# Two spare tiles in on-chip memory, and the first modulations on TensorE, in a two-block network on one core

## The chip, the core and the metric

The kernel runs on one core of a Trainium2 chip. TensorE (PE) does the matmuls, VectorE (DVE) and ScalarE (ACT) the elementwise work, GpSimd (POOL) a little of it, and SyncE (SP) issues nearly all transfers from one queue in program order. The metric is the device time of one execution in microseconds (us), lower is better. Before: median 3408.51 us of three runs (3404.82 to 3412.46).

## The reference

512 tokens of width 1024 pass through two blocks in float32. Every layer is modulated by a conditioning vector `c`: each needs a product of one vector with a 1024 x 3072 (first block) or 1024 x 6144 (second block) matrix before its activations can be scaled.

```python
def _modulation(c, w, b):
    m = jax.nn.silu(c) @ w + b
    shift, scale, gate = jnp.split(m, 3, axis=-1)
    return shift[:, None, :], scale[:, None, :], gate[:, None, :]

def first_block(...):
    for i in range(DEPTH):                       # DEPTH = 2
        shift, scale, gate = _modulation(c, mix_ada_w[i], mix_ada_b[i])
        h = x * (1.0 + scale) + shift
        y = _sgu_pool_mixer(h, ...) if i % 2 == 0 else _conformer_conv(h, ...)
        x = _layer_norm(DEEPNORM_ALPHA * x + (1.0 + gate) * y, mix_ln_g[i], mix_ln_b[i])
        shift, scale, gate = _modulation(c, ffn_ada_w[i], ffn_ada_b[i])
        h = x * (1.0 + scale) + shift
        y = _conv_ffn(h, ffn_w_up[i], ffn_dw[i], ffn_dw_b[i], ffn_w_down[i])
        x = _layer_norm(DEEPNORM_ALPHA * x + (1.0 + gate) * y, ffn_ln_g[i], ffn_ln_b[i])
    return x
# second_block: RWKV + windowed attention, then neighbourhood + global attention, with an FFN
# (width 4096) after each, modulated by six chunks each of silu(c_2) @ w_ada and silu(c_ctx_2) @ w_ada
```

The first mixer, `_sgu_pool_mixer`, projects to `u`, `v` and `z`, mixes `v` along the tokens, pools `z` over windows, and projects back.

## The kernel before

**Matmuls.** Activations are kept transposed (`hThi`, `hTlo`: 128 channels by 512 tokens for each of 8 channel groups). Every float32 product is taken in three fp32r matmuls, high by high, high by low and low by high (`mm3`, L304 to L308), and so each weight tile exists as `wraw` (as loaded), `whi` and `wlo` (pool `wp`). The names of the product's output tell the stage: `vps`, `ups`, `zps` and `dnps` in the first mixer, `upps` and `dnps` in the FFNs of block one, `cvps` and `cvacc` in the second mixer (`cvacc`: the depthwise convolution as matmuls with diagonal weights `dg`, 31 taps of three matmuls, each tap's moving operand starting 4 bytes further on), `up2ps` in block two.

**Where tiles lie.** Tiles are placed one behind the other in each partition's memory in the order in which pools make them. As the program is built, `whi`, `wlo` and `wraw` start 160 bytes past a multiple of 256, `hThi`, `hTlo` and the FFN's hidden tiles (`hidh`, `hidl`) 128 past one, `dg` 128 past one. A row names out <- moving operand, stationary operand: in `zps`, `ups`, `upps` and `up2ps` the activations move and the weights stand, in `vps` and `dnps` the weights move, and in `cvacc` the activations (`zh`, `zl`) move and `dg` stands.

**The modulations.** Before the first mixer can scale its input, `ada_first` (L251) computes shift and scale for the first half of the channels (q=0) and then for the second (q=1): four parts of 512 columns, each from two raw tiles of 1 MB (`adaw`, three in rotation). For a raw tile DVE multiplies four 128x512 slices by a per-partition scalar and adds them up (`ada_rows`, L202 and L204), and then TensorE sums over partitions with four 128x1 matmuls (`adaps`, L209). The other modulations of block one and those of block two are cut into pieces of 256 columns (`ada_piece`, two raws of 512 KB, two `adaw` buffers, three sums `adacc`), which are mixed into the stream by `fill()`: each call takes one entry of `todo` (L784). Twelve pieces lie in the first mixer: the gate of the mixer, then shift, scale and gate of the first FFN. SP issues a piece's transfer when its buffer is free, and every later transfer waits behind it.

Of the kernel before, what the change touches and what calls it, by code (L numbers as in the profile page):

```python
# [1 line left out]

# [3 lines left out]

# [5 lines left out]
F32 = mybir.dt.float32  # L12
# [9 lines left out]
D = 1024  # L22
KD = 8
# [19 lines left out]
class Consts:  # L43


    def __init__(self):
        self.parts, self.at, self.n = [], {}, 0
# [11 lines left out]
def host_consts():  # L59
    c0, c1, c2, c3, c4, c5, c6 = (Consts() for _ in range(7))  # L60
    p = np.arange(128)
    c0.put("ident", np.eye(128))
    c0.put("one", np.ones((128, 1)))
    c0.put("ones5", np.ones((128, 128)))
    c0.put("head", np.stack([p < 64, p >= 64], 1))

    c1.put("ones", np.ones((128, 128)))
    ic = np.ones((4, 2, 8), np.float32)
    for g, w in enumerate(WINDOWS):
        h = w // 2  # L70
        t = np.arange(S)
        c = (np.minimum(t + h, S) - np.maximum(t - h, 0)).astype(np.float32)
        ic[g, 0] = np.float32(1) / c[:8]
        ic[g, 1] = np.float32(1) / c[-8:]
    c1.put("ic", np.repeat(ic.reshape(1, 64), 128, 0))

    f = p % 64
    inv = (np.float32(ROPE_BASE) ** (-np.arange(16, dtype=np.float32) / np.float32(16))).astype(np.float32)
    t = np.arange(S)
    pos = np.where((f < 32)[:, None], t[None] // GRID_W, t[None] % GRID_W).astype(np.float32)  # L80
    ang = (pos * inv[f % 16][:, None]).astype(np.float32).astype(np.float64)
    c3.put("cos", np.cos(ang))
    c3.put("sin", np.sin(ang))
    perm = np.zeros((128, 128))
    for m in range(128):
        if m % 32 < 16:
            perm[m + 16, m] = -1
        else:
            perm[m - 16, m] = 1
    c3.put("perm", perm)  # L90

    q, k = np.arange(128)[:, None], np.arange(128)[None]
    c2.put("prev", np.where(k >= q, 0, NEG))
    c2.put("next", np.where(k <= q, 0, NEG))

    t, u = (p % 64)[:, None], np.arange(64)[None]
    c4.put("eye", t == u)
    c4.put("mn0", u < t)
    c4.put("mn1", u > t)
    c4.put("mq0", t <= u)  # L100
    c4.put("mq1", t >= u)
    c4.put("dg", t // 16 == u // 16)
    c4.put("lo", np.concatenate([(t // 16 > u // 16) & (p[:, None] // 64 == q) for q in range(2)], 1))
    c4.put("dg2", p[:, None] // 16 == p[None] // 16)

    c6.put("reset", np.repeat(np.arange(T2)[None] % 64 != 0, 128, 0))
    c6.put("heads", p[:, None] // 64 == p[None] // 64)

    t = p % 64
    c5.put("colmask", np.where((np.arange(64)[None] >= np.clip(t - 8, 0, 48)[:, None])  # L110
                               & (np.arange(64)[None] < np.clip(t - 8, 0, 48)[:, None] + 16), 0, NEG))
    return [c0, c1, c2, c3, c4, c5, c6]
# [7 lines left out]
class Kernel:  # L120
# [3 lines left out]
    todo = []  # L124
# [5 lines left out]
    def __init__(self, tc, ap, consts):  # L130
        self.tc, self.nc, self.ap = tc, tc.nc, ap
        self.consts = consts
        self.es = ExitStack()
        self.const = self.pool("const")
        self.wp = self.pool("wp")
        self.small = self.pool("small")
        self.nacc = self.pool("nacc")
        self.vp2 = self.pool("vec2")
        self.hp = self.pool("hT")
        self.vec, self.c = {}, {}  # L140
        self.load_consts(0, self.const)

    def pool(self, name, es=None, **k):
        return (es or self.es).enter_context(self.tc.tile_pool(name=name, bufs=1, reuse_waits="tile", **k))
# [44 lines left out]
    def silu_cols(self, name, vecs):  # L189
# [3 lines left out]
            self.nc.scalar.activation(t[:, m], v, AF.Silu)  # L193
        return t

    def ada_rows(self, acc, raw, sil, m, h):

        v = self.nc.vector
        for k in range(4):
            s = sil[:, m, h + k:h + k + 1]  # L200
            if h + k == 0:
                v.tensor_scalar(acc, raw[:, k, :], s, None, op0=MUL)  # L202
            else:
                v.scalar_tensor_tensor(acc, raw[:, k, :], s, acc, op0=MUL, op1=ADD)  # L204
# [6 lines left out]
    def ada_piece(self, w, sil, c0, dst, ms, buf, sums):  # L211
# [17 lines left out]
                nc.vector.tensor_copy(dst[:, ms[0]:ms[0] + n, c0 // 128:c0 // 128 + 2], t)  # L229
        return [partial(part, 0), partial(part, 4)]  # L230

    def ada_load(self, d, bias, pool):

        _, m, n = d.shape
        c = pool.tile([128, m, n], F32, tag=f"mod{m}{n}", name="mod", bufs=2)
        self.nc.vector.tensor_tensor(c, d, bias[:, None, :].to_broadcast([128, m, n]), ADD)
        return c
# [13 lines left out]
    def ada_first(self, w, sil, bias):  # L251

        nc = self.nc
        big = self.nacc.tile([128, 3, 4, 512], F32, tag="nacc", name="adaw0")
        m = self.vp.tile([128, 2, KD], F32, name="m0")
        i = 0
        for q in range(2):
            for x in range(2):
                acc = self.tmp("adacc0")
                c0 = D * x + 512 * q  # L260
                for h in (0, 4):
                    raw, i = big[:, i % 3], i + 1
                    nc.sync.dma_start(raw, w[128 * h:128 * h + 512, c0:c0 + 512].rearrange("(k p) c -> p k c", p=128))
                    self.ada_rows(acc, raw, sil, 0, h)
                t = self.ps.tile([128, 4], F32, tag="tr", name="adaps", bufs=2)
                self.ada_sums(t, acc)
                k = slice(4 * q, 4 * q + 4)
                nc.vector.tensor_tensor(m[:, x, k], t, bias[:, KD * x + 4 * q:KD * x + 4 * q + 4], ADD)
                if x == 1:
                    nc.vector.tensor_scalar(m[:, x, k], m[:, x, k], 1.0, None, op0=ADD)  # L270
            yield m
# [461 lines left out]
    def block1(self, xd):  # L733
        nc, ap = self.nc, self.ap
# [7 lines left out]
        adaw = lambda: self.act.tile([128, 4, 256], F32, tag="adaw", name="adaw", bufs=2)  # L742
        adaw()
        self.tmp("first", S + 16)
        x = self.act.tile([128, NT, D], F32, name="x")
        self.cols("a", [("c", ap["c"]), ("c2", ap["c_2"]), ("cc2", ap["c_ctx_2"])] + [(f"mix_b{i}", ap["mix_ada_b"][i]) for i in range(2)])
        sil = self.silu_cols("silc", [self.vec["c"]])
        self.sil2 = sil2 = self.silu_cols("sil2", [self.vec["c2"], self.vec["cc2"]])
        sums = lambda n: [self.vp.tile([128, 256], F32, tag="adacc", name="adacc", bufs=3) for _ in range(n)]
        ada1 = [self.vp.tile([128, 1, 3 * KD], F32, name=f"ada1_{k}") for k in range(4)]  # L750
        rows1 = self.tc.dram_tile([4, 1, D], F32, name="gates1")
        self.rows2 = self.tc.dram_tile([2, 2, 2, D], F32, name="gates2")
        self.ada_d = [self.vp2.tile([128, 2, 6 * KD], F32, name=f"ada2_{i}") for i in range(2)]
        V = self.vec
        first = self.ada_first(ap["mix_ada_w"][0], sil, V["mix_b0"])
        ws = []
        for q in range(2):
            m0 = next(first)
# [8 lines left out]
        n = x  # L767
        phases = [(i, part) for i in range(2) for part in ("mix", "ffn")]

        def ada(k, *qs):  # L770
            i, part = phases[k]
            pieces = [self.ada_piece(ap[f"{part}_ada_w"][i], sil, 512 * q + c, ada1[k], (0,), adaw, sums) for q in qs for c in (0, 256)]
            return [lambda p=p: [f() for f in p] for p in pieces]

        ada2 = [f for c in range(24) for f in self.ada_piece(ap["w_ada_2"][0], sil2, 256 * c, self.ada_d[0], (0, 1), adaw, sums)]

        def columns():
# [3 lines left out]
            self.cols("e", [("cv_dw", ap["cv_dw"]), ("cv_db", ap["cv_dw_b"]), ("cv_lng", ap["cv_ln_g"]),  # L781
                            ("cv_lnb", ap["cv_ln_b"])])

        todo = [ada(0,4,5)+[columns]+ada(1,0,1)+["gate"]+ada(1,2,3)+["mod"],  # L784
                ada(1, 4, 5) + ["gate"] + ada(2, 0, 1, 2, 3) + ["mod"] + ada(2, 4, 5) + ada(3, 0, 1, 2, 3, 4, 5) + ada2[:14],
                ["gate", "mod"],
                ["gate"] + ada2[14:] + self.begin2()]
        for k, (i, part) in enumerate(phases):
# [4 lines left out]
            rows = self.rows_gb(ap[f"{part}_ln_g"][i], ap[f"{part}_ln_b"][i])  # L793
            gate = self.act.tile([128, D], F32, tag="gate", name="gate", bufs=1)
# [23 lines left out]
            f = (lambda *a: self.ffn1(i, *a)) if part == "ffn" else (partial(self.mixer0, ws), self.mixer1)[i]  # L818
            n = f(hT, done, gate, x)
# [1165 lines left out]
```

## Time and profile before

| | before |
|---|---|
| median of three runs | 3408.51 us |
| the profiled execution | 3406.89 us |
| its span, first to last instruction | 3405.1 us |
| mean granted TensorE clock | 0.956 of 2.4 GHz |
| PE busy | 3149.5 us, 92% of the span |
| DVE busy | 2397.1 us, 70% |
| ACT busy | 1274.0 us, 37% |
| data moved | 435.41 MB, mean 128 GB/s |

The profiled execution lasts 1.8 us longer than its span and is 1.6 us below the median. Busy time is the union of an engine's instructions. A PE row's mean is the time from the start of one matmul to its end; matmuls overlap in the array, so what a stream costs is read from the distance between starts. 1.00 in a clock column is 2.4 GHz, 0.50 is 1.2 GHz.

### The profile page before, as it was taken

What the parts mean: (1) busy time and instruction counts of PE and PEld (TensorE: products, weight loads), DVE (VectorE), ACT (ScalarE), POOL (GpSimd) and SP (SyncE); (2) the same over time, 40 slices, a digit from 0 to 9 for tenths busy, and PEclk for the clock granted to TensorE, in tenths of its full rate; (3) what the DMA queues carried; (4) which work ended last, traced back from release to release, by engine and by line L of the source; (5) the groups of instructions that cost most, each with busy time, mean ns of one, the idle gap of its engine ahead of it and who ended that gap; (6) DMA issues with size and microseconds to landing.
All of it is one profiled execution on the core that took longest, in us unless ns stands there. A gap on an engine that the chain in (4) does not pass through costs nothing. (4 is left out here: it accounts for less than half of the span.)

```text
span 3405.1 us, 48625 instructions
## 1 busy us (share of the span) xinstructions
PE 3149.5 (92%) x18832; PEld 2611.5 (77%) x18832; DVE 2397.1 (70%) x4820; ACT 1274.0 (37%) x2094; POOL 298.2 (9%) x178
## 2 busy tenths in 40 slices
PE   6889999897999998988887999999999989999998
PEld 5677888775788877866677877888888777778886
DVE  7898888998878876787677679554664627763334
ACT  2233332345433335444623345222222526753222
POOL 0020000200200000132133201110000100010001
PEclk8889999998999998989988998999999999999999
DMA  7546754311344434346232245652442484143322
GB/s 240 185 125 216 216 167 142 112 44 44 112 150 140 139 103 120 112 121 188 61 92 64 63 146 168 173 147 91 152 141 68 131 226 152 38 164 97 93 94 80
DMA packets 518097, 435.41 MB, mean 128 GB/s; under 512 B 90628, under 2 KB 447722, under 8 KB 516330
## 3 DMA queue, kind: packets, MB, share of 16 engines
q1 hardware_dynamic: 517866, 432.30, 41.8%
q8 instruction: 148, 2.42, 0.3%
q14 instruction: 83, 0.68, 0.1%
HBM read 368.37 MB, written 63.22 MB: 127 GB/s over the span
## 5 line engine op out<-in xcount | busy, mean ns | idle before, releaser
L306 PE MATMUL dnps<-whi_dn,hidh 128*128 128x512 f32 x1120 | 446.7, 399 | 7.0 <-ACT hidh L281 3.0
L307 PE MATMUL dnps<-wlo_dn,hidh 128*128 128x512 f32 x1120 | 444.5, 397 | 1.4 <-DVE wlo_dn L294 1.4
L308 PE MATMUL dnps<-whi_dn,hidl 128*128 128x512 f32 x1120 | 442.7, 397 | 3.3 <-DVE hidl L282 3.1
L306 PE MATMUL upps<-hThi,whi_up 128*128 128x512 f32 (+1 forms) x768 | 296.6, 388 | 8.3 <-DVE hThi L281 8.3
L307 PE MATMUL upps<-hTlo,whi_up 128*128 128x512 f32 (+1 forms) x768 | 294.0, 384 | 6.3 <-DVE hTlo L282 6.3
L308 PE MATMUL upps<-hThi,wlo_up 128*128 128x512 f32 (+1 forms) x768 | 293.6, 383 | 0.0
L294 DVE TENSOR_TENSOR wlo_dn<-wraw_dn,whi_dn 128x1024 fp32r<-128x1024 f32 x140 | 170.8, 1222 | 147.2 <-ACT whi_dn L293 146.4
L204 DVE SCALAR_TENSOR_TENSOR adacc<-adaw,sil,adacc 128x256 f32<-128x256 f32 x560 | 262.9, 500 | 11.3 <-DMA adaw<-in_w_ada_dram 8.1
L306 PEld LDWEIGHTS dnps<-whi_dn,hidh 128*128 128x128 f32 x1120 | 210.7, 188 | 65.1 <-ACT hidh L281 6.0
L308 PEld LDWEIGHTS dnps<-whi_dn,hidl 128*128 128x128 f32 x1120 | 210.3, 188 | 56.3 <-DVE hidl L282 6.1
L307 PEld LDWEIGHTS dnps<-wlo_dn,hidh 128*128 128x128 f32 x1120 | 210.8, 188 | 52.0 <-DVE wlo_dn L294 2.3
L428 DVE TENSOR_TENSOR acc<-dnps,acc 128x512 f32<-128x512 f32 x200 | 136.8, 687 | 157.3 <-PE dnps L308 156.4
L293 ACT CAST whi_dn<-wraw_dn 128x1024 fp32r<-128x1024 f32 x140 | 146.8, 1049 | 259.3 <-PE up2ps L307 84.4
L307 PE MATMUL up2ps<-hTlo,whi_ff 128*128 128x512 f32 (+1 forms) x576 | 216.6, 376 | 5.3 <-DVE hTlo L282 4.0
L306 PE MATMUL up2ps<-hThi,whi_ff 128*128 128x512 f32 (+1 forms) x576 | 216.1, 377 | 2.7 <-DVE hThi L281 2.7
L308 PE MATMUL up2ps<-hThi,wlo_ff 128*128 128x512 f32 (+1 forms) x576 | 214.4, 373 | 0.0
L306 PEld LDWEIGHTS upps<-hThi,whi_up 128*128 128x128 f32 x768 | 147.7, 193 | 36.7 <-DVE hThi L281 9.6
L307 PEld LDWEIGHTS upps<-hTlo,whi_up 128*128 128x128 f32 x768 | 147.7, 193 | 34.6 <-DVE hTlo L282 7.8
L308 PEld LDWEIGHTS upps<-hThi,wlo_up 128*128 128x128 f32 x768 | 147.7, 193 | 29.1 <-DVE wlo_up L294 0.6
L204 DVE SCALAR_TENSOR_TENSOR adacc<-adaw,silc,adacc 128x256 f32<-128x256 f32 (+1 forms) x308 | 160.0, 521 | 12.1 <-DMA adaw<-in_ffn_ada_w_dram 4.3
L293 ACT CAST whi_ff<-wraw_ff 128x1024 fp32r<-128x1024 f32 x64 | 67.0, 1049 | 263.0 <-PE dnps L308 213.7
L294 DVE TENSOR_TENSOR wlo_ff<-wraw_ff,whi_ff 128x1024 fp32r<-128x1024 f32 x64 | 81.8, 1280 | 96.0 <-ACT whi_ff L293 95.5
(518 smaller groups left out, 7357.6 us busy)
## 6 DMA issues: line engine op xcount, KB each, us to landing
adaw<-in_w_ada_dram SPq DMA_DIRECT2D x96, 512.0 KB
wraw_up<-in_ffn_w_up_dram SPq DMA_DIRECT2D x88, 512.0 KB
wraw_ff<-in_w_ff_dram SPq DMA_DIRECT2D x64, 512.0 KB
wraw_dn<-in_w_ff_dram SPq DMA_DIRECT2D x64, 512.0 KB
adaw<-in_ffn_ada_w_dram SPq DMA_DIRECT2D x48, 512.0 KB
wraw_dn<-in_ffn_w_down_dram SPq DMA_DIRECT2D x44, 512.0 KB
adaw<-in_mix_ada_w_dram SPq DMA_DIRECT2D x32, 512.0 KB
ab<-ab SPq DMA_DIRECT2D x32, 384.0 KB
```

The costliest lines, as they stand in the source:

```text
L204: v.scalar_tensor_tensor(acc, raw[:, k, :], s, acc, op0=MUL, op1=ADD)
L293: nc.scalar.copy(hi, raw)
L294: (eng or nc.vector).tensor_tensor(lo, raw, hi, SUB)
L306: mm(out, a[0], b[0], start=first, stop=False)
L307: mm(out, a[0], b[1], start=False, stop=False)
L308: mm(out, a[1], b[0], start=False, stop=last)
L428: nc.vector.tensor_tensor(acc[:, t, c], p, acc[:, t, c], ADD)
```

## The change

Three things. **Spare tiles:** a tile of 96 bytes behind the first constants (`place0`, pool `const`) and one of 32 bytes in pool `vp2` (`place`); nothing reads or writes them. As built, `whi`, `wlo`, `wraw`, `hThi`, `hTlo`, `hidh`, `hidl`, `dg` and `adaw` then start at multiples of 256; `zh`, `zl` swap their 0 and 128; the accumulator `acc` goes from 0 to 96, and some attention tiles of block two (`kh`, `kl`, `qs`) from 96 to 224. **Modulation by matmul:** the four parts of `ada_first` and the twelve pieces of the first mixer (`early`) no longer use DVE for the products. The silu column of each channel group becomes a 128x32 stationary tile with one column used (`silw`), four channel groups go to four column positions of the array, and fp32 matmuls with the raw as the moving operand accumulate a 128 x 512 (or 256) PSUM tile, ACT copies it to `adarows`, and 128x1 matmuls with a 0/1 column (`sel`) add the four used rows (`adat`). **Sums:** the pieces that stay on DVE (from the first FFN on) have two `adacc` tiles in place of three.

```diff
+        self.const.tile([128, 24], F32, name="place0")
...
+    def silu_wide(self, src):
+        t = self.vp.tile([128, KD, 32], F32, name="silw")
+        self.nc.vector.memset(t, 0.0)
+        self.nc.vector.tensor_copy(t[:, :, 0], src[:, 0])
+        return t
...
+    def ada_part(self, w, sil, c0, t, raw):
+        nc = self.nc
+        n = 128 * t.shape[1]
+        acc = self.ps.tile([128, n], F32, tag="tr", name="adaps", bufs=2)
+        parts = [raw() for h in (0, 4)]
+        for h, r in zip((0, 4), parts):
+            nc.sync.dma_start(r, w[128 * h:128 * h + 512, c0:c0 + n].rearrange("(k p) c -> p k c", p=128))
+        for h, r in zip((0, 4), parts):
+            for k in range(4):
+                nc.tensor.matmul(acc[32 * k:32 * k + 32], sil[:, h + k, :], r[:, k, :], start=h == 0, stop=h > 0)
+        rows = self.tmp("adarows", n)
+        nc.scalar.copy(rows, acc)
+        for j in range(t.shape[1]):
+            nc.tensor.matmul(t[:, j:j + 1], rows[:, 128 * j:128 * j + 128], self.c["sel"], start=True, stop=True)
...
-                acc = self.tmp("adacc0")
-                    raw, i = big[:, i % 3], i + 1
-                    self.ada_rows(acc, raw, sil, 0, h)
-                t = self.ps.tile([128, 4], F32, tag="tr", name="adaps", bufs=2)
-                self.ada_sums(t, acc)
+                t = self.ps.tile([128, 4], F32, tag="tr", name="adat", bufs=2)
+                self.ada_part(w, sil, D * x + 512 * q, t, lambda: big[:, next(parts)])
...
-        sums = lambda n: [self.vp.tile([128, 256], F32, tag="adacc", name="adacc", bufs=3) for _ in range(n)]
+        sums = lambda n: [self.vp.tile([128, 256], F32, tag="adacc", name="adacc", bufs=2) for _ in range(n)]
...
+        self.vp2.tile([128, 8], F32, name="place")
...
-        todo = [ada(0,4,5)+[columns]+ada(1,0,1)+["gate"]+ada(1,2,3)+["mod"],
+        todo = [early(0,4,5)+[columns]+early(1,0,1)+["gate"]+early(1,2,3)+["mod"],
```

The order of the program moves too. On PE, in the stretch of the first mixer where `v` is mixed along the tokens (`mixps`), stood before:

```order
341 L542 MATMUL mixps<-wsT,acc 128x128 x4
342 L209 MATMUL adaps<-consts_73,adacc 128x1 x4
343 L542 MATMUL mixps<-wsT,acc 128x128 x4
344 L209 MATMUL adaps<-consts_73,adacc 128x1 x2
345 L584 MATMUL poolps<-pool,mixpw 128x512
```

and now stands, behind the same `zps` matmuls:

```order
359 L252 MATMUL adaps<-adaw,silw 32x256 x8
360 L256 MATMUL adat<-consts_73,adarows 128x1 x2
361 L567 MATMUL mixps<-wsT,acc 128x128 x4
362 L252 MATMUL adaps<-adaw,silw 32x256 x8
363 L256 MATMUL adat<-consts_73,adarows 128x1 x2
364 L252 MATMUL adaps<-adaw,silw 32x256 x8
365 L256 MATMUL adat<-consts_73,adarows 128x1 x2
366 L277 MATMUL gatet<-consts_73,mod 8x128
367 L252 MATMUL adaps<-adaw,silw 32x256 x4
368 L609 MATMUL poolps<-pool,mixpw 128x512
369 L252 MATMUL adaps<-adaw,silw 32x256 x4
370 L331 MATMUL zps<-hThi,whi_inz 128x512
```

Four pieces now follow each other on PE, each of which reads 1 MB that must have arrived. On PE the parts for the second half of the channels now stand inside the `vps` stream of the first half, with the raw as an operand of PE itself:

```order
19 L332 MATMUL vps<-wlo_inv,hThi 128x512
20 L252 MATMUL adaps<-adaw_122,silw 32x512 x4
21 L333 MATMUL vps<-whi_inv,hTlo 128x512
```

Before, only the 128x1 sums stood there. On SP the transfers of four pieces now stand in one run ahead of the last loads of the mixer's output weights:

```order
46 L314 DMA wraw_dn<-in_ab_w_out_dram 128x2x512
47 L1109 DMA sink<-in_b_sink_dram 128x8
48 L314 DMA wraw_dn<-in_ab_w_out_dram 128x2x512
49 L249 DMA adaw<-in_ffn_ada_w_dram 128x4x256 x8
50 L280 DMA gates_117<-gater 8x128
```

The two raws of a piece are issued together and take both buffers, so that the next piece's transfers wait for TensorE to have used these.

## Rows read from the trace of the kernel before

**Rows 1.** The page: spans, busy tenths in 40 slices, granted clock.

```profile
span 3405.1 us, 48625 instructions
PE 3149.5 (92%) x18832; PEld 2611.5 (77%) x18832; DVE 2397.1 (70%) x4820; ACT 1274.0 (37%) x2094; POOL 298.2 (9%) x178
PE   6889999897999998988887999999999989999998
...
PEclk8889999998999998989988998999999999999999
```

**Rows 2.** Stretches: us, busy us (x instructions) by engine, PE clock, DMA share, GB/s.

```profile
0.00:24.00 24.00, 4.09 (x18) 3.84 (x19) 11.71 (x18) 1.89 (x5) 0.20 (x4) 1.00 0.87 325
105.00:135.00 30.00, 19.92 (x82) 15.77 (x81) 22.29 (x63) 5.00 (x12) 0.00 (x0) 0.72 0.49 152
135.00:205.00 70.00, 64.07 (x268) 49.26 (x266) 66.00 (x141) 15.28 (x17) 4.73 (x2) 0.98 0.50 159
205.00:620.00 415.00, 397.36 (x1846) 324.97 (x1847) 359.82 (x687) 142.34 (x182) 15.77 (x7) 0.97 0.57 174
```

**Rows 3.** L306 over the whole span, same columns (PE, PEld, clock, DMA share, GB/s).

```profile
0.00:3405.00 3405.00, 1457.33 (x3890) 743.96 (x3890) 0.96 0.42 128
```

**Rows 4.** Timeline of PE: start, length, one matmul of `zps`, of `dnps` and of `ups` each.

```profile
104.05 0.40 PE L306 MATMUL zps<-hThi,whi_inz 128*128 128x512 f32 x1
...
107.08 0.40 PE L307 MATMUL zps<-hTlo,whi_inz 128*128 128x512 f32 x1
...
834.74 0.40 PE L308 MATMUL dnps<-whi_dn,hidl 128*128 128x512 f32 x1
...
840.80 0.40 PE L307 MATMUL dnps<-wlo_dn,hidh 128*128 128x512 f32 x1
...
103.22 0.28 PE L308 MATMUL ups<-hThi,wlo_inu 128*128 128x256 f32 x1
...
103.93 0.28 PE L308 MATMUL ups<-hThi,wlo_inu 128*128 128x256 f32 x1
```

**Rows 5.** The convolution's tile: durations ns min/median/max; start us of the first and last.

```profile
L306 PE MATMUL cvacc<-zh,dg x74: 387/393/494, 717.3 to 790.7; 128*128 128x512 f32 x74
```

**Rows 6.** Timeline of PE: two `cvacc` taps, up to the next matmul.

```profile
719.78 0.40 PE L306 MATMUL cvacc<-zh,dg 128*128 128x512 f32 x1
...
721.17 0.39 PE L308 MATMUL cvps<-hThi,wlo_cvin 128*128 128x512 f32 x1
```

**Rows 7.** PE's waits from 0 to 205 us: total, times, longest.

```profile
PE adaps L209 <- DVE adacc L204: 31.0, 7, 9.5
```

**Rows 8.** Timeline of DVE: parts of `ada_first`.

```profile
8.57 0.49 DVE L202 TENSOR_SCALAR adacc<-adaw,silc 128x512 f32<-128x512 f32 x1 [3.16 <-DMA adaw<-in_mix_ada_w_dram]
9.09 5.48 DVE L204 SCALAR_TENSOR_TENSOR adacc<-adaw,silc,adacc 128x512 f32<-128x512 f32 x7
16.60 5.47 DVE L204 SCALAR_TENSOR_TENSOR adacc<-adaw,silc,adacc 128x512 f32<-128x512 f32 x7
```

**Rows 9.** Timeline of PE: start of the first mixer's stages, with the idle before.

```profile
27.96 1.22 PE L306 MATMUL vps<-whi_inv,hThi 128*128 128x512 f32 x2 [0.25 <-ACT whi_inv L293]
...
46.85 1.84 PE L209 MATMUL adaps<-consts,adacc 128*128 128x1 f32 x8 [4.22 <-DVE adacc L204]
...
73.26 0.98 PE L209 MATMUL adaps<-consts,adacc 128*128 128x1 f32 x4 [4.73 <-DVE adacc L204]
...
77.03 0.41 PE L307 MATMUL ups<-hTlo,whi_inu 128*128 128x256 f32 x1
...
79.38 0.41 PE L306 MATMUL ups<-hThi,whi_inu 128*128 128x256 f32 x1
...
116.58 2.05 PE L542 MATMUL mixps<-wsT,acc 128*128 128x128 f32 x8
124.49 0.99 PE L209 MATMUL adaps<-consts,adacc 128*128 128x1 f32 x4 [5.85 <-DVE adacc L204]
126.88 2.05 PE L584 MATMUL poolps<-pool,mixpw 128*128 128x512 f32 x2 [1.41 <-DVE pool L580]
```

**Rows 10.** Timeline of PE: matmuls with a 64-column stationary (two records each).

```profile
2832.31 1.53 PE L327 MATMUL o<-scratchhTlo,cv 128*64 128x128 f32 x24
```

**Rows 11.** DVE by group and shape, 0 to 205 us: count, busy us, mean ns.

```profile
L204 DVE SCALAR_TENSOR_TENSOR adacc<-adaw,silc,adacc 128x256 f32<-128x256 f32 x95 | 46.9, 496 | 5.6 <-DMA adaw<-in_ffn_ada_w_dram 4.0 <-DMA adaw<-in_mix_ada_w_dram 0.8
```

**Rows 12.** Timeline of SP: issue of the first four raws of 1 MB.

```profile
3.48 8.33 SPq L263 DMA_DIRECT2D adaw<-in_mix_ada_w_dram  x4
```

**Rows 13.** DVE's waits from 205 to 620 us.

```profile
DVE ada L229 <- PE adaps L209: 11.5, 15, 2.8
```

More of the change, by code (lines that the diff above doesn't have):

```diff
@@ L4 @@
 from functools import partial
-from itertools import zip_longest
+from itertools import cycle, zip_longest
 import concourse.bacc as bacc
@@ L63, in host_consts @@
     c0.put("one", np.ones((128, 1)))
+    c0.put("sel", (p % 32 == 0)[:, None])
     c0.put("ones5", np.ones((128, 128)))
@@ L230, in ada_piece, with ada_early @@
         return [partial(part, 0), partial(part, 4)]
+    def ada_part(self, w, sil, c0, t, raw):
[12 more added lines that the diff above has]
+            nc.tensor.matmul(t[:, j:j + 1], rows[:, 128 * j:128 * j + 128], self.c["sel"], start=True, stop=True)
+    def ada_early(self, w, sil, c0, dst, raw):
+        t = self.ps.tile([128, 2], F32, tag="tr", name="adat", bufs=2)
+        self.ada_part(w, sil, c0, t, raw)
+        self.nc.vector.tensor_copy(dst[:, c0 // 128:c0 // 128 + 2], t)
     def ada_load(self, d, bias, pool):
@@ L255, in ada_first @@
         m = self.vp.tile([128, 2, KD], F32, name="m0")
-        i = 0
+        parts = cycle(range(3))
         for q in range(2):
             for x in range(2):
-                acc = self.tmp("adacc0")
-                c0 = D * x + 512 * q
-                for h in (0, 4):
-                    raw, i = big[:, i % 3], i + 1
-                    nc.sync.dma_start(raw, w[128 * h:128 * h + 512, c0:c0 + 512].rearrange("(k p) c -> p k c", p=128))
-                    self.ada_rows(acc, raw, sil, 0, h)
-                t = self.ps.tile([128, 4], F32, tag="tr", name="adaps", bufs=2)
-                self.ada_sums(t, acc)
+                t = self.ps.tile([128, 4], F32, tag="tr", name="adat", bufs=2)
+                self.ada_part(w, sil, D * x + 512 * q, t, lambda: big[:, next(parts)])
                 k = slice(4 * q, 4 * q + 4)
@@ L747, in block1 @@
         sil = self.silu_cols("silc", [self.vec["c"]])
+        silw = self.silu_wide(sil)
         self.sil2 = sil2 = self.silu_cols("sil2", [self.vec["c2"], self.vec["cc2"]])
-        sums = lambda n: [self.vp.tile([128, 256], F32, tag="adacc", name="adacc", bufs=3) for _ in range(n)]
+        sums = lambda n: [self.vp.tile([128, 256], F32, tag="adacc", name="adacc", bufs=2) for _ in range(n)]
         ada1 = [self.vp.tile([128, 1, 3 * KD], F32, name=f"ada1_{k}") for k in range(4)]
@@ L752, in block1 @@
         self.rows2 = self.tc.dram_tile([2, 2, 2, D], F32, name="gates2")
+        self.vp2.tile([128, 8], F32, name="place")
         self.ada_d = [self.vp2.tile([128, 2, 6 * KD], F32, name=f"ada2_{i}") for i in range(2)]
         V = self.vec
-        first = self.ada_first(ap["mix_ada_w"][0], sil, V["mix_b0"])
+        first = self.ada_first(ap["mix_ada_w"][0], silw, V["mix_b0"])
         ws = []
@@ L773, in ada, with early @@
             return [lambda p=p: [f() for f in p] for p in pieces]
+        def early(k, *qs):
+            i, part = phases[k]
+            return [partial(self.ada_early, ap[f"{part}_ada_w"][i], silw, 512 * q + c, ada1[k][:, 0], adaw) for q in qs for c in (0, 256)]
         ada2 = [f for c in range(24) for f in self.ada_piece(ap["w_ada_2"][0], sil2, 256 * c, self.ada_d[0], (0, 1), adaw, sums)]
```

## The prediction

> **What bounds the kernel.** I read the page first, then stretches, then groups by shape, then waits and timelines. TensorE is busy in 92% of the span, nothing else above 70% [rows 1], and where its busy share falls its granted clock falls too. So there are two ways to save time: make the matmuls themselves shorter, everywhere, or remove idle time and low clock in the few stretches that have them. The spare tiles aim at the first, the modulations at the second.
>
> The matmuls: each of the three lines of the split product has 3,890 of them [rows 3], of which I count over the groups by shape some 2,870 of 512 columns and 1,020 of 256. Starts are 0.2331 us apart in `zps` (13 steps in 3.03 us) and 0.2331 in `dnps` (26 in 6.06); in `ups` with 256 columns 0.1183 (6 in 0.71) [rows 4]. That gives 3 x 2,870 x 0.2332 + 3 x 1,020 x 0.1183 = 2,008 + 362 = 2,370 us, 70% of the span. One per cent of it is 24 us, which is more than all that the modulations can give. So the price of an address is the main unknown.
>
> **Part 1, the spare tiles.** They cost no instruction. What do they buy? The trace of before has three arrangements. In `zps` the moving operand starts 128 bytes past a multiple of 256 and the stationary one 160; in `dnps` the moving one 160, the stationary one 128. Both step at 0.2331 [rows 4]. If an odd 32 bytes in the operand that is streamed cost anything, these would differ, and they don't. In the convolution the stationary tile is at 128 and the moving one at any multiple of 4: six matmuls in 1.39 us, 0.2317 each, 0.6% shorter [rows 6], with durations from 387 to 403 ns about a median of 393 (the longer ones are few: 494 at the top is a start from a standstill) [rows 5]. So there is a difference of a few ns from one address to another, but no row has both operands at a multiple of 256, and none shows that more alignment is better. The bounds: none at all (as `zps` against `dnps` say), to 387 against 393 for every matmul, 6 of 233 ns or 2.6%, 61 us; on the other side the convolution's durations spread above their median too, most of them by less than 10 ns, and I bound a loss by a third of that, 3 ns or 1.3% (31 us). I take the one measured step between two arrangements, 0.6% of 2,370: **-13 us**, nearer to nothing than to the far end, since it is the row nearest to what the change makes. The same shift moves what DVE and ACT read and write; their rows show no pair that differs in address alone, so I add nothing.
>
> **Part 2, the modulations.** Removed from DVE: the four parts, each 0.49 + 5.47 us [rows 8] and one more multiply, and for the twelve pieces 8 instructions of 0.496 us each [rows 11], 12 x 8 x 0.496 = 48 us. DVE is not the bound over the whole, but in the first mixer it is: 66.0 of 70 us from 135 to 205 [rows 2], and TensorE waits 31.0 us for `adacc` before 205 us, seven times [rows 7].
>
> Added to TensorE: 8 matmuls in fp32 a part or piece with a stationary of 32 columns. No row has such a tile; the nearest has 64 columns and 128 moving columns: 24 records, that is 12 instructions, in 1.53 us, so 0.11 each after the last one's 0.27 us [rows 10]. For 512 columns that is 0.44 us, for 256 0.22. A part then costs 3.5 us, a piece 1.76, at full clock, and double at 1.2 GHz. Bounds: a quarter of it (the four column positions run side by side) to all of it doubled. The 128x1 sums stay the same in number.
>
> The Trainium skill (TensorE: Matmul & The Clock Gate, Part 3: Packing small matmuls) says that matmuls at different column positions run concurrently, and gives 2.38 times for three of them. The rows just used alternate between two column positions and show none of it. By the page a part would cost about an estimated 1.5 us and not 3.5.
>
> Now along TensorE's order.
> - To the first `vps` at 27.96 us [rows 9]. Raws arrive as before; the fourth is issued when the first has been used, 11.8 us [rows 12], which for TensorE at half clock is no earlier. Then 3.5 us and a copy replace 5.5 us of DVE [rows 8], and x and the first weights must have come too. Gain 2 us (0 to 4).
> - The second half: before, TensorE waits 4.22 us and then starts at half clock [rows 9]. After, the parts stand inside the `vps` stream, as the order shows, so that the wait goes, 4.2 us, and 3 us of slow matmuls behind it; but 2 x 3.5 us of new matmuls come in. Net 0.
> - At 73.26 us a wait of 4.73 us goes, and behind it `ups` matmuls 0.214 us apart (11 from 77.03 to 79.38) where 0.118 is normal [rows 9]: 25 or so of them, 2.5 us. Gain 7.
> - The twelve pieces add 12 x 1.76 = 21 us. Four of them stand where TensorE idled already, from `mixps` to `poolps`: waits of 5.85 and 1.41 us in the stretch from 105 to 135, of which it was busy 19.9 of 30 us at a clock of 0.72 [rows 2, 9]. These 7 us are free there, if nothing else is late. What is late next is the pieces' own data: a first raw took from its issue at 3.48 to its use at 8.57, 5.1 us [rows 8, 12], and the next piece's transfer waits for TensorE to be done with the former one. I set that against the DVE waits that go: no gain, no loss here. The other eight pieces cost 14 us.
> - DVE is 94% busy from 135 to 205 and TensorE idle 6 us [rows 2]. Some of the 48 us taken from DVE lies there; I take half of TensorE's idle time: gain 3.
>
> Sum: -2 + 0 - 7 + 14 - 3 = **+2 us**, with 10 less if the column positions overlap and 15 more if the pieces' data hold TensorE up.
>
> **Part 3, two sums.** In the first FFN DVE waits 11.5 us for `adaps`, 15 times [rows 13], and with two buffers a piece that needs two must wait for the one before. DVE is busy 360 of 415 us there and TensorE 397 [rows 2], so that most of it is covered by DVE's own slack: **+1 us** (0 to 8).
>
> Sum: -13 + 2 + 1 = -10 us on the profiled 3406.9, that is 3397; the median shown is 1.6 us above that execution. About 0.2% (7 us) is what a measurement of this kernel can tell from no change, so this forecast lies just beyond it.
>
> **The rivals.**
> - *Alignment counts in full.* For it: the spread of the convolution's durations shows that an address can be worth 6 ns. Against: `zps` and `dnps` agree to a tenth of a nanosecond with different operands off. Price: -61 + 3, so 3349.
> - *Alignment is worth nothing, and the modulations only move the wait.* Then +3 on 3406.9: 3410. For it: the equality of `zps` and `dnps`. This is also the case in which the change doesn't do what it says.
> - *The pieces' transfers hold TensorE up* (slower). Place: the three pieces behind `mixps` and the next one, in order on TensorE, each needing 1 MB whose issue waits for the piece before. Price: 3 x (5.1 + 1.76) = 20.6 us, where before from the end of `mixps` at 118.6 to `poolps` at 126.9 there were 8.3 [rows 9], so +12; the clock, already at 0.72, stays low into the following `zps`, +3. SP's queue holds the output weights behind them too. It decides when a piece's 1 MB takes more than the 2 us or so that other work on TensorE covers. With no gain from alignment 3425, with 13 of it 3412.
> - *Column positions overlap.* For it: a full tile of 128 columns would have more to do in fp32 than the 0.11 us of these rows, so that a narrow tile does leave part of the array to others. Against: the rows alternate between two positions and start one after the other [rows 10]. At a quarter of the price the pieces cost 5 and not 21 us, of which 14 lay on the path: about 10 us less, 3387. The rule of the Trainium skill named above (TensorE: Matmul & The Clock Gate, Part 3) would have it so.
>
> **How the numbers follow.** My forecast, some gain from alignment and the modulations about even: 0.35. Alignment in full or most of it (3345 to 3375): 0.2. Nothing from alignment, modulations even: 0.2. Transfers hold TensorE up without a gain: 0.15. Overlap, with little from alignment: 0.1. The forecast's own range is 3385 to 3408. To leave no more than 2 in 10 outside, the range goes from 3350 to 3420. Faster by over 0.2% (below 3401.7): 0.35 x 0.7 + 0.2 + 0.2 x 0.2 + 0.1 x 0.85 = 0.57. Slower (above 3415.3): 0.15 x 0.75 + 0.2 x 0.25 + 0.35 x 0.05 = 0.18. Within: 0.25.
>
> **What would show it.** The distance between starts in `zps`, `dnps` and `up2ps`: 0.2331 again means that alignment is nothing, 0.2315 is my case, 0.227 the full one. The wait of 31.0 us for `adacc` before 205 us gone, and in its place waits of `adaps` for the transfer of `adaw`: under 10 us for my case, 20 for the slow rival. Eight matmuls of `adaps` with 32x256 in 1.8 us, or in 0.5 if they overlap. The first mixer's end at 205 within 5 us. Wrong would be the whole reasoning if `dnps` became slower, or if DVE's or ACT's rows change length by address.

## The result and the profile after

The changed kernel takes 3368.16 us (median of four runs, 3363.85 to 3372.57), the kernel before on the same chip 3407.07 us: a ratio of 0.9884, 95% interval 0.9865 to 0.9902, or 39 us less. The forecast was 3397 in a range of 3350 to 3420, with the sign right and the size a quarter of what came.

The page of the profiled execution (span, busy time, granted clock) answers to [rows 1]:

```profile
span 3362.1 us, 49040 instructions
PE 3125.3 (93%) x19088; PEld 2605.2 (77%) x19088; DVE 2327.8 (69%) x4694; ACT 1279.1 (38%) x2110; POOL 300.2 (9%) x178
...
PEclk9999999898999998998988999999999999999999
```

The span is 43.0 us shorter. TensorE has 256 more records and is yet busy 24 us less; the clock digits of the first three slices have gone from 8 to 9 (of the later ones two rise and two fall; the mean granted clock goes from 0.956 to 0.962). So both roads that the prediction named were taken: shorter matmuls and a better start.

**The steps.** The timeline of PE, a stream of `dnps` from its first shown row to its last, 28 steps, then a stream of 256 columns, 14 steps; they answer to [rows 4]:

```profile
3249.81 0.39 PE L332 MATMUL dnps<-wlo_dn,hidh 128*128 128x512 f32 x1
...
3256.16 0.39 PE L333 MATMUL dnps<-whi_dn,hidl 128*128 128x512 f32 x1
...
2099.77 0.28 PE L331 MATMUL up2ps<-hTchi,whi_ff 128*128 128x256 f32 x1
...
2101.45 0.28 PE L333 MATMUL up2ps<-hTchi,wlo_ff 128*128 128x256 f32 x1
```

6.35 us over 28 is 0.2268 where 0.2331 was; 1.68 over 14 is 0.1200 where 0.1183 was. Over all steps of a stream that lie within a tenth of their median the means are 227.2 ns for `dnps` (before 233.3), 227.5 for `up2ps` (233.2), and 119.7 for 256 columns (118.4). The long ones became 2.6% shorter, the short ones 1.1% longer.

**The first mixer.** PE's waits of the changed kernel from 24 to 205 us, which answer to [rows 7]:

```profile
PE adaps L252 <- DMA adaw<-in_ffn_ada_w_dram: 4.7, 7, 1.8
PE upps L332 <- DVE hTlo L307: 3.7, 3, 1.8
PE upps L331 <- DVE hThi L306: 1.8, 1, 1.8
PE adat L256 <- ACT adarows L254: 1.6, 3, 0.5
```

The 31.0 us of waiting for `adacc` are gone, 15.9 of which lay behind 24 us. What replaced these 15.9 is 4.7 us of waiting for the pieces' own data, seven times; ahead of 24 us, where TensorE has little else to do, it waits 4.5 us for the raws of `ada_first`. The timeline of PE shows the place of [rows 9] where the pieces follow one another, and ahead of it one piece in the `ups` stream:

```profile
61.92 1.07 PE L252 MATMUL adaps<-adaw,silw 128*32 128x256 f32 x16
...
108.17 0.64 PE L252 MATMUL adaps<-adaw,silw 128*32 128x256 f32 x8 [0.55 <-DMA adaw<-in_ffn_ada_w_dram]
109.95 0.64 PE L252 MATMUL adaps<-adaw,silw 128*32 128x256 f32 x8 [1.14 <-DMA adaw<-in_ffn_ada_w_dram]
...
115.22 1.08 PE L252 MATMUL adaps<-adaw,silw 128*32 128x256 f32 x8 [1.77 <-DMA adaw<-in_ffn_ada_w_dram]
116.85 1.01 PE L256 MATMUL adat<-consts,adarows 128*128 128x1 f32 x4 [0.55 <-ACT adarows L254]
...
119.93 2.08 PE L609 MATMUL poolps<-pool,mixpw 128*128 128x512 f32 x2 [0.58 <-DVE mixz L586]
```

A whole piece is 16 records in 1.07 us at full clock; the longest wait for data is 1.77 us. From the end of `mixps` (107.6) to `poolps` there are 12.3 us where 8.3 were: longer, as the slow rival said, but not its 20.6, and the stretch begins 11 us earlier and ends 7 us earlier. The stretches (columns as in [rows 2]):

```profile
24.00:62.00 38.00, 36.44 (x182) 24.58 (x185) 22.41 (x74) 17.25 (x27) 0.00 (x0) 1.00 0.69 232
62.00:94.80 32.80, 32.80 (x294) 29.16 (x295) 17.49 (x40) 9.33 (x14) 0.00 (x0) 1.00 0.78 238
94.80:130.70 35.90, 29.03 (x186) 17.34 (x184) 13.46 (x35) 9.71 (x21) 0.00 (x0) 0.81 0.59 194
```

TensorE is now busy all through the `ups` stream, at full clock, and the stretch behind it, with the pieces in a row, still has a low clock, 0.81. Where each stage's first matmul starts, us from the span's start, in this execution and in those of the two parts run alone (below):

| first matmul of | before | changed | tiles alone | modulations alone |
|---|---|---|---|---|
| `vps` | 28.0 | 24.8 | 28.2 | 24.6 |
| `ups` | 66.3 | 62.9 | 66.8 | 62.6 |
| `zps` | 104.0 | 94.8 | 104.8 | 94.8 |
| `dnps` | 149.6 | 130.7 | 150.8 | 130.9 |
| `upps`, first FFN | 213.6 | 197.1 | 214.4 | 198.5 |
| `cvps`, second mixer | 635.9 | 614.9 | 630.2 | 625.4 |
| `upps`, second FFN | 877.9 | 856.8 | 871.7 | 870.2 |
| `up2ps`, second block | 1291.1 | 1268.5 | 1282.5 | 1288.6 |
| `up2ps`, its first FFN | 2071.6 | 2048.8 | 2065.7 | 2074.4 |
| `dps` behind that FFN | 2681.2 | 2648.9 | 2665.9 | 2682.1 |
| `up2ps`, its second FFN | 3026.0 | 2991.8 | 3007.0 | 3026.0 |
| end of the last matmul | 3395.4 | 3352.0 | 3367.8 | 3394.6 |

### The profile page after: what moved, and what is told of

The parts are those of the page before. It is cut to its first block, busy times and chain, and to the rows that moved or that the text cites. A ratio compares the mean times of both kernels' runs of the same rounds, so it can differ in the third digit from the quotient of the medians.

```text
span 3362.1 us, 49040 instructions
## 1 busy us (share of the span) xinstructions
PE 3125.3 (93%) x19088; PEld 2605.2 (77%) x19088; DVE 2327.8 (69%) x4694; ACT 1279.1 (38%) x2110; POOL 300.2 (9%) x178
## 5 line engine op out<-in xcount | busy, mean ns | idle before, releaser
L213 DVE SCALAR_TENSOR_TENSOR adacc<-adaw,sil,adacc 128x256 f32<-128x256 f32 x560 | 255.5, 498 | 6.2 <-DMA adaw<-in_w_ada_dram 4.3
L453 DVE TENSOR_TENSOR acc<-dnps,acc 128x512 f32<-128x512 f32 x200 | 136.7, 687 | 151.7 <-PE dnps L333 150.8
L332 PE MATMUL up2ps<-hTlo,whi_ff 128*128 128x512 f32 (+1 forms) x576 | 213.6, 371 | 4.7 <-DVE hTlo L307 4.0
L875 POOL TENSOR_TENSOR ag<-acc,gg 128x1024 f32<-128x1024 f32 x20 | 49.2, 2458 | 1101.7 <-DVE acc L453 1070.5
```

Source lines behind the costliest of these rows:

```text
L332: mm(out, a[0], b[1], start=False, stop=False)
L453: nc.vector.tensor_tensor(acc[:, t, c], p, acc[:, t, c], ADD)
L875: nc.gpsimd.tensor_tensor(ag, a, gg[:, 0 if t < NT else 1, :], MUL)
```

## The experiments

**1. The spare tiles alone.** The kernel before with

```diff
         self.load_consts(0, self.const)
+        self.const.tile([128, 24], F32, name="place0")
...
+        self.vp2.tile([128, 8], F32, name="place")
```

> The kernel before with the two spare tiles alone; the modulations stay on VectorE with three sums. If the starting addresses made the matmuls shorter, the 512-column ones step at about 227.3 ns as in the changed kernel (233.2 before), the 256-column ones at 119.7 (118.4 before), and the time is about 3383 us: the 43 us that the change gave less the 19 us gained by the end of the first mixer. If the shorter steps come from something else (VectorE less busy), they stay at 233.2 and the time at 3407.

Measured: 3379.58 us, ratio 0.9910 (0.9895 to 0.9926); 227.2 and 227.5 ns for 512 columns, 119.7 for 256. The same stretch of `dnps` as above, 28 steps in 6.35 us:

```profile
3249.78 0.39 PE L308 MATMUL dnps<-wlo_dn,hidh 128*128 128x512 f32 x1
...
3256.13 0.39 PE L309 MATMUL dnps<-whi_dn,hidl 128*128 128x512 f32 x1
```

So two tiles that nothing reads give 31 us of 3413 by the ratio (the medians differ by 34), and nothing else in the program has changed but where tiles lie. The other engines and the transfers did not get faster by it: the splits of the `dn` weights have medians of 1225 ns on VectorE and 1048 on ScalarE before, 1224 and 1053 here, and a DMA packet of 2048 bytes has a median of 84 ns in both traces.

**2. The modulations alone.** The changed kernel without the two tiles.

```diff
-        self.const.tile([128, 24], F32, name="place0")
...
-        self.vp2.tile([128, 8], F32, name="place")
```

> The changed kernel without the two spare tiles: the modulations of the first mixer on TensorE and two sums, at the addresses of before. If the two parts are independent: 233.2 ns for 512 columns, the first FFN begins some 15 us earlier than before (213.6), and the time is about 3390 us. If the two sums cost in the first FFN, part of the 15 us is lost again by the start of the second mixer (635.9 before).

Measured: 3403.10 us, 0.9973 (0.9964 to 0.9982), 9 us less by the ratio, where 17 were expected; steps as before (233.3 and 233.2). 0.9910 times 0.9973 is 0.9883, the changed kernel's 0.9884: the parts add up. The first FFN begins 15.1 us earlier, as the changed one nearly does, but the table shows part of it lost again: 10.5 us remain at the second mixer, 7.7 at the second FFN, 2.5 at the second block and 0.8 at the end. The table overstates this: its column is an execution of 3406.11 us, 3 above the median, on a chip on which the kernel before takes 3413 us, while the column of before is from the first chip, with 3407. By the ratio 9 of the 15 us are left.

**3 to 8. Which addresses.** All are other sizes of the two tiles, in floats of a partition; no computation changes. First, only one kind of operand on a multiple of 256 (weights, then inputs and hidden tiles):

```diff
+        self.const.tile([128, 24], F32, name="place0")
+        self.vp2.tile([128, 40], F32, name="place")
```

> The kernel before with spare tiles of 96 and 160 bytes: the weights start at multiples of 256, transposed inputs and hidden tiles 128 past one, as before. If only the odd 32 bytes in the weights' address cost (theory A: a multiple of 64 or 128 is enough): 227.3 ns everywhere and about 3383 us. If both operands must start on a multiple of 256 (theory B), or at the same offset within 256 (theory C): 233 ns and 3407 us.

```diff
-        self.const.tile([128, 24], F32, name="place0")
-        self.vp2.tile([128, 8], F32, name="place")
+        self.vp2.tile([128, 32], F32, name="place")
```

> The changed kernel with one spare tile of 128 bytes in the second place: weights 160 past a multiple of 256 as before, transposed inputs and hidden tiles on multiples of 256. Theories A, B and C (odd 32 bytes; both on 256; same offset) all give 233 ns and about 3390 us; if the inputs alone count (theory D), 227.3 ns and 3368 us.

Then both kinds at the same offset, which is not zero (56 and 8 floats, 40 and 8, 32 and 8):

> The kernel before with spare tiles of 224 and 32 bytes: weights, transposed inputs and hidden tiles all start 128 past a multiple of 256. Theory B (both operands on multiples of 256): 233 ns for 512 columns and about 3407 us. Theory C (both at the same offset within 256, as the convolution's first taps in the two traces hint): 227.3 ns and about 3380 us. The odd 32 bytes alone are out already, since weights on 256 with inputs on 128 step at 232.6.

> The kernel before with spare tiles of 160 and 32 bytes: all of these 64 past a multiple of 256. Theory B: 233 ns, 3407 us. Theory C: 227.3 ns, 3380 us. If the grid is 128 and not 256 with equal offsets, 128 past is fast and this is not.

> The kernel before with spare tiles of 128 and 32 bytes: all of these 32 past a multiple of 256, while kh, kl and qs of block two come to lie on multiples of 256. Theory B: 233 ns for the large products, 3407 us, and 227 for the attention's 512-column scores (232 to 233 in all runs so far). Theory C: 227.3 ns, 3380 us.

And a difference of 64 (24 and 24 floats):

> The kernel before with spare tiles of 96 and 96 bytes: weights on multiples of 256, transposed inputs and hidden tiles 64 past one, so that the two operands differ by 64. If only equal offsets within 256 help: 232.5 to 233.5 ns for 512 columns and 3407 us. If a difference of 64 is as good as none, which the convolution's steps hint at (227.9 ns over 36 of them at that difference): 227.5 ns and 3382 us.

Measured, with the start of weights (W) and of inputs and hidden tiles (H) past a multiple of 256; "difference" is moving less stationary within 256, in the down products (weights move) and the up products (inputs move); steps in ns, means as above; the up columns are those of `up2ps`:

| run | W, H | difference down, up | down 512 | up 512 | up 256 | ratio (95%) |
|---|---|---|---|---|---|---|
| before | 160, 128 | 32, 224 | 233.3 | 233.2 | 118.4 | 1 |
| tiles alone | 0, 0 | 0, 0 | 227.2 | 227.5 | 119.7 | 0.9910 (0.9895 to 0.9926) |
| w128_h128 | 128, 128 | 0, 0 | 227.1 | 227.5 | 119.7 | 0.9912 (0.9896 to 0.9928) |
| w64_h64 | 64, 64 | 0, 0 | 227.1 | 227.4 | 119.7 | 0.9933 (0.9914 to 0.9951) |
| w32_h32 | 32, 32 | 0, 0 | 227.2 | 227.5 | 119.7 | 0.9935 (0.9916 to 0.9954) |
| w0_h64 | 0, 64 | 192, 64 | 233.3 | 230.0 | 116.2 | 0.9958 (0.9945 to 0.9971) |
| w0_h128 | 0, 128 | 128, 128 | 232.7 | 232.7 | 119.1 | 0.9988 (0.9979 to 0.9997) |
| w160_h0 (changed modulations) | 160, 0 | 160, 96 | 234.2 | 233.5 | 119.9 | 0.9982 (0.9971 to 0.9993) |

The timelines of the runs at 32 and 32 (29 steps in 6.58 us, 0.2269) and at 0 and 128 (28 in 6.50, 0.2321):

```profile
3249.69 0.39 PE L308 MATMUL dnps<-wlo_dn,hidh 128*128 128x512 f32 x1
...
3256.27 0.39 PE L307 MATMUL dnps<-whi_dn,hidh 128*128 128x512 f32 x1
```

```profile
3249.78 0.40 PE L308 MATMUL up2ps<-hTlo,whi_ff 128*128 128x512 f32 x1
...
3256.28 0.40 PE L309 MATMUL up2ps<-hThi,wlo_ff 128*128 128x512 f32 x1
```

Theory A (odd 32 bytes), theory B (multiples of 256) and theory D (the inputs alone) fall; theory C stands for the streams of split products: **the two operands have to start at the same offset within 256 bytes, whatever it is.** Multiples of 256 are one way to get it. A difference of 64 helps in part, 230.0 with the moving operand 64 ahead and 233.3 with it 64 behind, which neither reading of that run had said; the first is from the up products and the second from the down products, and no run tells the direction from the kind of product. In the run at 160 and 0, the modulations are those of the changed kernel, and its time is 3406.69 us, like that of the modulations alone and not the 3390 expected. Equal offsets are not enough everywhere: the attention's scores of 512 columns, `kh`, `kl` and `qs` all on multiples of 256 in the run at 32, still step at 233.7, as at 232 to 233 in every run, although their offsets are always equal. They are not one stream but four short matmuls between others; why they don't gain is open. The runs at 64 and 32 are some 10 us slower than those at 0 and 128 with the same steps; in the one at 64, 6 us of it lie in the first FFN (422.1 us from `upps` to `cvps` against 415.8 with the tiles alone), where TensorE waits more for `adacc` (6.1 against 3.0 us). That is not the length of the matmuls; what else it is stays open.

**9. Only the low weights apart.** A tile of 128 bytes between the high and the low weights, and one of 160 in the second place:

```diff
-        hi, lo = tile(0, F32R), tile(1, F32R)
+        hi = tile(0, F32R)
+        if not self.gap:
+            self.gap = self.wp.tile([128, 32], F32, name="gap")
+        lo = tile(1, F32R)
...
+        self.vp2.tile([128, 40], F32, name="place")
```

> The kernel before with a spare tile of 128 bytes between the high and the low weights and one of 160 in the second place: whi, hThi, hTlo, hidh, hidl all 160 past a multiple of 256, wlo alone 32 past one, so that only pairs with wlo differ, by 128. Two ways to read equal offsets. If a matmul's moving operand has to match its own stationary one: in the up products the step from the third matmul of a split product (wlo stands) to the next is 232.7 ns and the other two 227; in the down products the step from the second (wlo moves). If it has to match the stationary one that is loaded meanwhile for the next matmul: in the up products the step from the second is the long one, in the down products the second too. Time about 3390 us in both.

Measured: 3403.23 us, 0.9969 (0.9958 to 0.9980), where 3390 was expected. Mean steps from the first, second and third matmul of a split product: in the up products 227.7, 232.3 and 233.8 ns, in the down products 231.4, 232.5 and 229.8. Two products of an up stream, 6 steps in 1.39 us:

```profile
3302.51 0.39 PE L310 MATMUL up2ps<-hThi,whi_ff 128*128 128x512 f32 x1
...
3303.90 0.39 PE L310 MATMUL up2ps<-hThi,whi_ff 128*128 128x512 f32 x1
```

Each reading said that one step of three is long. Two are in the up products: the one in which the low weights are loaded behind the second matmul, and the one in which they stand. All three are in the down products. Both readings fall as the only rule. In the up products the step without any part of `wlo` keeps its 227.7. In the down products the third step has none either (the high weights move, `hidl` stands, `hidh` is loaded for the next, all three at 160) and takes 229.8, so a rule by pairs of operands does not account for it. That the relation counts and not an address by itself rests on the table above; which of the operands in flight have to agree stays open.

**10 to 12. The third sum.** The changed kernel with three `adacc` again; `silw` lives in the first of them while the early pieces need it, so that no address moves. Beside it, in a second measurement, the changed kernel once more on the same chip.

```diff
-        t = self.vp.tile([128, KD, 32], F32, name="silw")
+        t = self.vp.tile([128, 256], F32, tag="adacc", name="silw", bufs=3).rearrange("p (k c) -> p k c", k=KD)
...
-        sums = lambda n: [self.vp.tile([128, 256], F32, tag="adacc", name="adacc", bufs=2) for _ in range(n)]
+        sums = lambda n: [self.vp.tile([128, 256], F32, tag="adacc", name="adacc", bufs=3) for _ in range(n)]
```

> The changed kernel with three sums again, the first of which holds the silu stationary while the early pieces need it, so that no more memory is used and every address stays. If the third sum is what the FFNs of block one lost (4.6 us in the first and 5 in the second, modulations alone against before), the time is some 8 us below the changed kernel's, 3360 us, and VectorE's waits for the sums' matmuls in the second FFN (2.4 us for a free sum) go. If the sums don't matter, 3368.

> The changed kernel itself, beside its variant with three sums on the same chip: 0.988 of the kernel before.

> The variant with three sums again, beside the changed kernel on the same chip. If the third sum is worth the 8 us that the first look showed in the two FFNs, its ratio to the kernel before lies 0.002 to 0.003 below that of the changed kernel; if that was scatter between runs, within 0.001.

Measured: three sums 3362.44 us, 0.9852 (0.9828 to 0.9875), then 3364.47, 0.9864 (0.9842 to 0.9886); the changed kernel beside the second 3368.57, 0.9873 (0.9857 to 0.9890). 4 us apart on the same chip, with intervals that overlap and ratios only 0.0009 apart, which the expectation called scatter: the times don't settle it. The traces of both pairs agree for the FFNs. From `upps` to `cvps` the changed kernel takes 417.8 and 420.0 us, with three sums 413.6 and 414.4; the second FFN 411.7 and 413.5 against 407.3 and 406.7. DVE's waits in the second FFN, first of the changed kernel, then with three sums:

```profile
DVE wlo_dn L319 <- ACT whi_dn L318: 13.9, 11, 3.7
DVE ada L238 <- PE adaps L218: 3.7, 7, 0.7
DVE adacc L211 <- PE adaps L218: 2.4, 3, 1.5
```

```profile
DVE wlo_dn L319 <- ACT whi_dn L318: 7.4, 10, 1.8
DVE ada L238 <- PE adaps L218: 6.8, 13, 0.7
DVE adacc L213 <- DMA adaw<-in_w_ada_dram: 4.0, 3, 1.7
```

With two sums a multiply waits until TensorE has read the older sum (2.4 us), and the low weights wait longer; with three the row `adacc` <- `adaps` is gone, and a multiply waits for a transfer instead. How this reaches TensorE is not shown: no row of that FFN has it waiting for `wlo_dn`, its idle time falls from 18.7 to 16.8 us, and its busy time from 393.0 to 390.6, at a granted clock of 0.97 and 0.98. So by the traces the third sum is worth 4 to 7 us in each FFN; 3 us of that are given back ahead of the first (from `dnps` to `upps` 70.1 and 69.9 us against 66.4 and 67.4), and the net was 4 us in the times beside each other, 8 to 10 in the spans.

## Why the prediction was right, and where its steps were off

The sign and the range held, since the largest term of the sum had the right sign; its size and that of the next one were off. In this the range was lucky: the 3368 us lie outside the forecast's own 3385 to 3408, and inside 3345 to 3375, the case of alignment in full or most of it, which had a chance of 0.2. Of the signs that were to show it, the step said the full case (0.227), the waits of the pieces the forecast (4.7 us), and the end of the first mixer, within 5 us by the forecast, came early: the first FFN begins 16.5 us sooner.

**The spare tiles (-13 forecast, -31 measured).** The mechanism was that an address can shorten every matmul; the size was wrong. The step that failed is "the one measured step between two arrangements, 0.6%" (of 2,370 us that is 14): it compared rows by how well each operand was aligned, and the streams gave 2.6%. `zps` and `dnps` in [rows 4] agree not because addresses don't matter but because in both the operands differ by 32 bytes, one way or the other; with the tiles alone they step at 228.6 and 227.2 ns.

The trace of before could not have given the price. It had more than the three arrangements: the attention's scores have both operands 96 past a multiple of 256 there, and step at 232. And the convolution of [rows 6], sorted by the difference of its operands within 256 bytes, gives 227.5 ns at 0 (four steps) but 225.3 at 224 (three) and 226.0 at 144 (two). Why its steps scatter, and why it was faster on the average, is open.

**Where the rest of it went.** The rival "alignment counts in full" had the step right (0.227) and the time wrong (3349). The steps alone would give 3 x 2,870 x 5.9 ns, or 51 us, less 3 x 1,020 x 1.3 = 4 us for the shorter matmuls that became slower, that is 47; the tiles alone gave 31. The table of stages shows where: the FFNs of the second block take 9.4 and 8.7 us less, all that their matmuls lost. The second FFN of block one takes 2.4 us less, though its 512-column steps sum to 8.2 us less: there TensorE waits more, for `hidh` 3.5 us where 0.6 were, and for `whi_dn` 1.5 where 0.7 were. Here a shorter matmul was worth its length only where TensorE alone was the limit.

**The modulations (+2 forecast, -9 measured).** By its steps, changed kernel against before: to the first `vps` -3.2 us (forecast -2); the second half -0.1 (0); the `ups` stream -5.9, `zps` -9.7, from `dnps` on +2.4, together -13.2, where the forecast had -7 + 14 - 3 = +4. The order moved 24 of the 72 `zps` matmuls from ahead of the first `dnps` to behind it, some 5.5 us, so that by the work these last two are about -4 and -3.

Two steps failed. One is the price of a piece, 1.76 us: it is 1.07 at full clock with the tail (the timeline above), so that twelve cost 13 and not 21 us. Of the eight that were counted, 14 becomes 9, which is 5 of the 17 us. The other is the stretch from the first `zps` to the first `dnps`, put at "no gain, no loss". The prediction set the waits of 5.85 and 1.41 us there against the pieces. TensorE idled 14.5 us of the 45.6 before and idles 6.9 of 35.9 now: the wait for `adacc` went, and with it a wait of 4.0 us for sums behind VectorE's `pool` and one of 2.3 us for a transfer, while the waits for data are 4.7 us in all. How the rest splits no run shows. By the first FFN that made -16.5 us. What the forecast didn't have is that part of it is lost later: of the 15.1 us of the modulations alone 9 are left by the ratio.

**Two sums (+1 forecast).** The bound of 0 to 8 held for the first FFN alone (4 to 6 us), but the second pays as much, and the term spoke only of the first. By the traces it is the largest part of that loss: the two FFNs lost 4.6 and 5.2 us with the modulations alone, as much as the third sum gave back to them; the times are too close to confirm it.

**The rivals.** The transfers held TensorE up for 4.7 us and not for 15; with no wait above 1.8 us, most of a raw's 5.1 us had passed when TensorE came to it. Column positions do overlap, in pairs (below): of that rival's 16 us (twelve pieces at 5 and not 21) 8 came, and of its 10 on the path 5. "Nothing from alignment" is out.

## What to carry to other kernels

Look at where a matmul's two operands start, relative to each other, and not at how round each address is: here equal offsets within 256 bytes took 2.6% from the step of the 512-column fp32r matmuls in the long streams for 128 bytes of memory, and tiles of other sizes (96 and 160 bytes, ratio 0.9988) gave nearly none of it. A step between starts that is the same in two streams is no proof of a floor: here both were off by the same 32 bytes, and moving one operand by a spare tile showed it. And when an engine is relieved, look for the buffer that paid for it: without the third sum, 1 KB in a partition, the FFNs took 4 to 7 us longer each in the traces.

## What the runs showed of the hardware that I had not expected

At full clock, in the streams of split products, the 512-column fp32r step was 227.1 to 227.5 ns with the operands at equal offsets within 256 bytes (0, 32, 64 and 128 alike), 230.0 with the moving one 64 ahead (up products), and 232.7 to 234.2 at the other differences tried. The short runs of the attention's scores stayed at 232 to 234 at equal offsets. At 256 columns the same offsets gave 119.7, 116.2 and 118.4 to 119.9, so that what was best for one was not best for the other.

An fp32 matmul with a 32-column stationary starts as two records 6 to 7 ns apart, and the next one, at the neighbouring column position, 6 to 7 ns behind; the third and fourth follow 0.22 us later as another such pair. A raw of four 256-column matmuls so takes the array 0.44 us, two at a time. The 64-column ones of [rows 10] alternate between two positions and don't overlap. The rule of the Trainium skill (TensorE: Matmul & The Clock Gate, Part 3: Packing small matmuls), that column positions run concurrently, is borne out in part here: pairs of 32 (8 matmuls of a piece in 1.07 us), none of 64, in fp32.
